# One-hot operands of a gate matrix made for eight tokens at a time, in slots shared with two tiles of the heads' stage

## Chip, cores and metric

The kernel runs on one core of one Trainium2 chip. The metric is the device time of one execution in microseconds (us). PE is TensorE, DVE is VectorE, ACT is ScalarE, POOL is GpSimd, and SP is the engine whose queue issues most of the DMAs.

## What is computed

One decoder block over 512 tokens of width 1024: a mixer (a depthwise convolution beside a sliding-window attention), and then a channel mixer that picks experts by product keys. The change lies in the second part, in float32 throughout:

```
def peer(h, w_pq, sub_keys, u_emb, v_emb):
    q = (h @ w_pq).reshape(B, S, PEER_HEADS, 2, PEER_DHALF)
    sc = jnp.einsum("bshcd,hcnd->bshcn", q, sub_keys)
    s_top, i_top = lax.top_k(sc, PEER_TOPK)                 # 16 of 128, twice per head
    cand = s_top[..., 0, :, None] + s_top[..., 1, None, :]
    cand_idx = i_top[..., 0, :, None] * N_KEYS + i_top[..., 1, None, :]
    best, pos = lax.top_k(cand, PEER_TOPK)                  # 16 of 256, per head
    expert_idx = jnp.take_along_axis(cand_idx, pos, axis=-1)
    gate = jax.nn.softmax(best, axis=-1)
    ...
    a = gelu(jnp.einsum("ced,cd->ce", u_emb[idx], hx))      # per token: 8 heads x 16 experts of 16384
    return jnp.einsum("ce,ced->cd", g * a, v_emb[idx])
```

## The kernel before

The 512 tokens are four blocks of 128. Block 0 takes its experts row by row: `gathered` (L634) fetches 128 rows of a table by an indirect DMA on POOL's queue, and DVE multiplies them (L651, L659). The other three blocks are dense: the product of all 16384 experts with all 384 tokens is formed on PE in 128 steps (`u_pieces`, L671, 24 matmuls of 384 columns each, with the weights split into a high and a low part by `load_w`, L128), multiplied by a gate matrix G, and multiplied with the second table (`v_products`, L698). G holds, for each token, the gate of each expert, and is nearly all zero.

The stages after the mixer, in order of time:

- **Heads** (`head`, L529, called eight times, 488 to 679 us). `scores` forms the queries (tile `pq`, L521, from PSUM by ACT) and multiplies them with the keys; DVE finds the top 16 (`top16`); `pick` (L548) looks the winners up through a one-hot tile `eq` (L569, one slot, twice per head) of 1024 elements per partition. Between the heads PE works on the first 25 `u_pieces`.
- **Gate stage** (`build_g`, L599, 684 to 847 us). Per block, `keys` (L584) transposes the indices, and `build_g` walks the 128 tokens. For each token G's 128 x 128 matrix is a product of two one-hot operands on PE (L628): `yt` marks the second key of each of the 128 chosen experts, `xt` the first key times the gate. DVE makes both: `yt` at L620 for `XT` = 4 tokens at once (512 elements per partition), `xt` at L623 likewise as a product of two narrow tiles `xa` and `xb`, which are made for 32 tokens at once (L612 twice, L614) in one slot each. `yt` and `xt` have two slots each (`XB` = 2). The four products of a group go to one PSUM tile of tag `sc` (two banks), ACT copies it into `gst` (L630), and after 16 tokens `gst` goes to DRAM (`gb`, L632, two slots). The choice between the tags `sc` and `ot` (L626) depends on the position within `XT` tokens in steps of four, so with four tokens it is always `sc`. After each group of four tokens 3.6 matmuls of the further `u_pieces` are threaded in (`U_PIECE`), so PE's queue alternates between a group of L628 and three or four matmuls of L146.
- **Loop over 128 steps** (from 847 us to the end). Per step: one `u_pieces`, a load of G's slice (`gl`, L685), its product with the experts' outputs (L690, L694, L695), `v_products` (L701 to L703), and about one gathered row of block 0 for DVE.

A scheduler orders the instructions of each engine at build time, and each engine runs its list in that order. Tiles are placed in pools; when the pools of the heads and the gate stage (`gp`, `rt`) are closed, the pools of the loop (`vp` with `gl`, `wh`, `wl`; `rows` with `hrow`, `acc` and the four slots of `row`) take the same memory, and a tile of theirs may be written once the tiles that lay there are released.

## Time and profile before

| | us |
|---|---|
| median of 3 runs | 1781.72 (1778.0 to 1785.92) |
| the profiled execution | 1780.86 |
| its span in the trace | 1779.1 |
| gate stage, first to last matmul of L628 | 684.1 to 845.9 |
| PE idle before matmuls of L628 | 12.2 |

The time of an execution holds its span and 1.8 us around it. A stage is read from the windows and the timeline: an engine's idle time there has a releaser in brackets, the instruction of another engine that ended it.

### The profile page before, as it was taken

To read this page: it belongs to the slowest core of one execution; us is meant where nothing else is said; L and a number is where in the kernel's file an instruction comes from. 1 tells how busy PE (TensorE), PEld (TensorE's weight loads), DVE (VectorE), ACT (ScalarE), POOL (GpSimd) and SP (SyncE) were. 2 spreads that over 40 slices of the span, in tenths; PEclk is the share of its full clock that TensorE was granted. 3 is DMA by queue.
4 is the path that set the end of the run, shared out by engine and by line. 5 is a ranking of instruction groups with operands and counts; after the bars stand their busy time and mean duration, and the time that the engine had idled before them with its cause. 6 is when DMAs were issued, how large, how long until landed. Compare 5 with 4: busy or idle time off the path is not lost. (4 is left out here: it accounts for less than half of the span.)

```text
span 1779.1 us, 25055 instructions
## 1 busy us (share of the span) xinstructions
PE 1708.0 (96%) x8892; PEld 1501.4 (84%) x8892; DVE 1366.0 (77%) x2755; ACT 905.6 (51%) x1287; POOL 458.6 (26%) x374
## 2 busy tenths in 40 slices
PE   7999999999999996999999999999999999989996
PEld 6887767788899996899999999999999999977775
DVE  6999994546689998888677777777768777768775
ACT  6449998644656656777333333333333333333332
POOL 1111010110111110001234434433535434434320
PEclk9999998999999998999999999999999999999998
DMA  8996553885999995878888889889979889878873
GB/s 243 229 220 152 131 129 74 188 225 177 259 217 218 212 210 153 257 240 263 300 318 316 318 282 325 316 287 321 322 275 326 309 295 337 302 267 302 299 259 127
DMA packets 165709, 444.86 MB, mean 250 GB/s; under 512 B 14544, under 2 KB 66256, under 8 KB 162512
## 3 DMA queue, kind: packets, MB, share of 16 engines
q0 software_dynamic: 53280, 194.01, 40.9%
q1 hardware_dynamic: 112304, 249.26, 39.2%
q8 instruction: 70, 1.15, 0.2%
q14 instruction: 55, 0.45, 0.1%
HBM read 410.44 MB, written 29.88 MB: 248 GB/s over the span
## 5 line engine op out<-in xcount | busy, mean ns | idle before, releaser
L131 ACT ACTIVATE whi<-wraw 128x1024 fp32r<-128x1024 f32 x346 | 365.3, 1057 | 358.1 <-PE mm L146 200.4
L146 PE MATMUL mm<-tTh,whi 128*128 128x384 f32 (+2 forms) x1168 | 398.5, 342 | 1.5 <-ACT wlo L134 1.4
L146 PE MATMUL mm<-tTl,whi 128*128 128x384 f32 (+2 forms) x1168 | 398.7, 342 | 0.2 <-DVE tTl L194 0.2
L137 DVE TENSOR_TENSOR wlo<-wraw,whi 128x1024 fp32r<-128x1024 f32 x232 | 282.5, 1221 | 63.1 <-ACT whi L131 55.9
L636 POOL DMA_INDIRECT row<-pv,eidx x128 | 181.2, 1416 | 275.9 <-DVE acc L659 259.9
L636 POOL DMA_INDIRECT row<-pu,eidx x128 | 178.2, 1392 | 265.4 <-DVE row L651 250.5
L694 ACT ACTIVATE wh<-gl 128x384 fp32r<-128x384 f32 x128 | 67.2, 526 | 345.8 <-PE ot L702 324.4
L146 PE MATMUL mm<-tTh,wlo 128*128 128x384 f32 (+2 forms) x1168 | 240.5, 341 | 0.0
L146 PEld LDWEIGHTS mm<-tTh,whi 128*128 128x128 f32 x1168 | 219.9, 188 | 9.9 <-ACT wlo L134 1.8
L146 PEld LDWEIGHTS mm<-tTl,whi 128*128 128x128 f32 x1168 | 219.8, 188 | 8.3 <-DVE tTl L194 0.4
L146 PEld LDWEIGHTS mm<-tTh,wlo 128*128 128x128 f32 x1168 | 202.9, 188 | 3.9
L659 DVE SCALAR_TENSOR_TENSOR acc<-row,gate,acc 128x1024 f32<-128x1024 f32 x128 | 163.9, 1280 | 12.9 <-DMA row<-pv,eidx 9.3
L296 DVE SCALAR_TENSOR_TENSOR yconv<-uc,pc,yconv 128x512 f32<-128x512 f32 x240 | 168.6, 741 | 0.4
L651 DVE SCALAR_TENSOR_TENSOR row<-row,hrow 128x1024 f32<-128x1024 f32 x128 | 154.2, 1219 | 7.7 <-DMA row<-pu,eidx 7.4
L146 PE MATMUL mm<-hTh,whi 128*128 128x512 f32 (+1 forms) x352 | 136.4, 390 | 1.1 <-ACT hTh L193 0.9
L146 PE MATMUL mm<-hTl,whi 128*128 128x512 f32 (+1 forms) x352 | 135.7, 388 | 1.4 <-DVE hTl L194 1.4
L695 DVE TENSOR_TENSOR wl<-gl,wh 128x384 fp32r<-128x384 f32 x128 | 70.9, 554 | 76.6 <-ACT wh L694 76.6
L134 ACT ACTIVATE wlo<-whi 128x1024 fp32r<-128x1024 f32 x114 | 120.1, 1054 | 9.7 <-PE mm L146 9.0
L690 DVE TENSOR_TENSOR gl<-gl,ga 128x384 f32<-128x384 f32 x128 | 61.9, 552 | 80.5 <-DMA gl<-gb 80.5
L630 ACT ACTIVATE gst<-sc 128x512 f32<-128x512 f32 x96 | 100.9, 1075 | 33.8 <-PE sc L628 27.7
L628 PE MATMUL sc<-xt,yt 128*128 128x128 f32 x768 | 103.2, 278 | 12.2 <-DVE xt L623 9.3
L628 PEld LDWEIGHTS sc<-xt,yt 128*128 128x128 f32 x768 | 99.1, 193 | 16.3 <-ACT gst L630 10.2
(252 smaller groups left out, 3107.9 us busy)
## 6 DMA issues: line engine op xcount, KB each, us to landing
wraw<-put SPq DMA_DIRECT2D x128, 512.0 KB, 5.5
wraw<-pv SPq DMA_DIRECT2D x128, 512.0 KB, 5.8
gb<-gst SPq DMA_DIRECT2D x24, 1024.0 KB, 5.5
gl<-gb SPq DMA_DIRECT2D x48, 512.0 KB, 7.1
wraw<-w_in SPq DMA_DIRECT2D x42, 512.0 KB, 4.8
wlo<-put POOLq DMA_DIRECT2D x42, 512.0 KB, 7.2
wlo<-w_in POOLq DMA_DIRECT2D x40, 512.0 KB, 6.0
wraw<-w_out SPq DMA_DIRECT2D x16, 512.0 KB, 3.4
```

Of the source, the lines that this page charges most:

```text
L131: nc.scalar.activation(hi, raw, AF.Copy)
L134: nc.scalar.activation(lo, hi.bitcast(F32), AF.Copy, scale=-1.0)
L137: nc.vector.tensor_tensor(lo, raw, hi.bitcast(F32), op=OP.subtract)
L146: pace[0] = nc.tensor.matmul(p, v[:, k * P:(k + 1) * P], t, start=(n == 0), stop=(n == len(terms) - 1))
L296: nc.vector.scalar_tensor_tensor(y[:, j], uc[:, t:t + S], w, y[:, j], op0=OP.mult, op1=OP.add)
L628: nc.tensor.matmul(p[:, t], yt[:, t1 + t], xt[:, t1 + t].rearrange("p a b -> p (a b)"), start=True, stop=True)
L630: nc.scalar.activation(st[:, :, t0 + t1:t0 + t1 + 4].rearrange("p i t -> p t i"), p, AF.Copy)
L636: ins = nc.gpsimd.indirect_dma_start(out=r, out_offset=None, in_=table, in_offset=bass.IndirectOffsetOnAxis(ap=eidx[:, ROW_CHUNKS.index(b) ...
L651: nc.vector.scalar_tensor_tensor(r, r, 1.0, h, op0=OP.mult, op1=OP.mult, accum_out=dots[:, s:s + 1])
L659: nc.vector.scalar_tensor_tensor(acc, r, gate[:, b, s:s + 1], acc, op0=OP.mult, op1=OP.add)
L694: nc.scalar.activation(wh3, w, AF.Copy)
L695: nc.vector.tensor_tensor(wl3, w, wh3.bitcast(F32), op=OP.subtract)
```

## The change

`XT` becomes 8: one instruction of DVE makes `yt` for eight tokens, one makes `xt`, of 1024 elements per partition each. The inner loop over steps of four tokens then runs twice per group, so the PSUM tiles alternate between `sc` and `ot`, two banks each. `yt` and `xt` keep two slots, of 4 KB per partition each instead of 2 KB. To make room, the heads' `pq` takes the slots of `xt`, and `eq` the slots of `yt` (two, where it had one); the memory of both pools together stays the same, but the tiles' places in it move.

```
-XT = 4
+XT = 8
...
-        q = rt.tile([P, S], F32, name="pq", bufs=2)
+        q = gp.tile([P, S], F32, name="pq", tag="xt", bufs=XB)
...
-            eq = rt.tile(wide, F32, name="eq")
+            eq = gp.tile(wide, F32, name="eq", tag="yt", bufs=XB)
...
-                yt = gp.tile([P, XT, P], F32, name="yt", bufs=XB)
+                yt = gp.tile([P, XT, P], F32, name="yt", tag="yt", bufs=XB)
...
-                xt = gp.tile([P, XT, high, LOW], F32, name="xt", bufs=XB)
+                xt = gp.tile([P, XT, high, LOW], F32, name="xt", tag="xt", bufs=XB)
```

The places move as follows, in bytes of a partition: `xt` and `yt` now lie at 176896 to 193280, in front of `xa`, `xb` and `gst` (`gst` at 196352 to 212736, before at 179968 to 196352). The first slot of `gl` (176896 to 189184) lay over `xa`, `xb` and both slots of `gst`, and lies now over `xt` and the first slot of `yt`. `hrow` and `acc` (207616 to 211712) and the first slot of `row` (211712 to 215808) lay over tiles of the heads, and lie now over the second slot of `gst` (and `sel`).

DVE's list at the third border between two blocks of 32 tokens (`xa` and `xb` belong to the new block). Before:

```order
L620 TENSOR_TENSOR yt<-keyT,iota 128x512
L623 TENSOR_TENSOR xt<-xa,xb 128x512
L612 TENSOR_TENSOR xa<-keyT,iota 128x256
L612 TENSOR_TENSOR xb<-keyT,iota 128x512
L620 TENSOR_TENSOR yt<-keyT,iota 128x512
L614 TENSOR_TENSOR xa<-xa,gT 128x256
L620 TENSOR_TENSOR yt<-keyT,iota 128x512
L623 TENSOR_TENSOR xt<-xa,xb 128x512 x2
```

The same place in the changed kernel:

```order
L620 TENSOR_TENSOR yt<-keyT,iota 128x1024
L623 TENSOR_TENSOR xt<-xa,xb 128x1024
L612 TENSOR_TENSOR xa<-keyT,iota 128x256
L612 TENSOR_TENSOR xb<-keyT,iota 128x512
L620 TENSOR_TENSOR yt<-keyT,iota 128x1024
L614 TENSOR_TENSOR xa<-xa,gT 128x256
L623 TENSOR_TENSOR xt<-xa,xb 128x1024
L620 TENSOR_TENSOR yt<-keyT,iota 128x1024
```

Before, two `yt` stand ahead of the block's first `xt` at each of the eleven borders of the stage (at five of them one stands ahead of `xa` already); now one does. PE's list keeps its order; only the PSUM tags alternate.

DVE's list at the start of the gate stage, before:

```order
L612 TENSOR_TENSOR xa<-keyT,iota 128x256
L612 TENSOR_TENSOR xb<-keyT,iota 128x512
L620 TENSOR_TENSOR yt<-keyT,iota 128x512 x2
L592 CAST k_p<-k_u 128x128
L614 TENSOR_TENSOR xa<-xa,gT 128x256
L593 SCALAR_TENSOR_TENSOR k_q<-k_p,sel 128x128
L623 TENSOR_TENSOR xt<-xa,xb 128x512 x2
```

In the changed kernel:

```order
L612 TENSOR_TENSOR xa<-keyT,iota 128x256
L612 TENSOR_TENSOR xb<-keyT,iota 128x512
L620 TENSOR_TENSOR yt<-keyT,iota 128x1024 x2
L592 CAST k_p<-k_u 128x128
L614 TENSOR_TENSOR xa<-xa,gT 128x256
L593 SCALAR_TENSOR_TENSOR k_q<-k_p,sel 128x128
L623 TENSOR_TENSOR xt<-xa,xb 128x1024 x2
```

The order is the same, each `yt` and `xt` being twice as long; PE's first L628 waits for the first `xt` of this list.

SP's queue at the end of the gate stage, before:

```order
L632 DMA gb_82<-gst 128x2048 x2
L125 DMA wraw<-put 128x1024
L647 DMA hrow<-h2d_79 128x1024
L632 DMA gb_82<-gst 128x2048 x2
L125 DMA wraw<-pv 128x1024
L632 DMA gb_82<-gst 128x2048
L125 DMA wraw<-put 128x1024
L685 DMA gl<-gb_80 128x8x128
L685 DMA gl<-gb_81 128x8x128
L685 DMA gl<-gb_82 128x8x128
```

In the changed kernel (`gb_80`, `gb_81` and `gb_82` are the gate matrices of the three blocks in DRAM, `h2d_79` block 0's input):

```order
L632 DMA gb_82<-gst 128x2048 x2
L125 DMA wraw<-put 128x1024
L632 DMA gb_82<-gst 128x2048 x2
L125 DMA wraw<-pv 128x1024
L632 DMA gb_82<-gst 128x2048
L125 DMA wraw<-put 128x1024
L685 DMA gl<-gb_80 128x8x128
L685 DMA gl<-gb_81 128x8x128
L685 DMA gl<-gb_82 128x8x128
L647 DMA hrow<-h2d_79 128x1024
```

The load of `hrow` moves from before the last three stores of the gate matrix to behind its first three loads.

## Rows read from the trace of the kernel before

**Rows 1.** The page's part 1, busy time of each engine over the whole span, its share of the span, and its instructions.

```profile
PE 1708.0 (96%) x8892; PEld 1501.4 (84%) x8892; DVE 1366.0 (77%) x2755; ACT 905.6 (51%) x1287; POOL 458.6 (26%) x374
```

**Rows 2.** Busy time of each engine by stretch: from and to, length, then PE, PEld, DVE, ACT and POOL with their instructions, the granted TensorE clock, the DMA engines' share and GB/s. The first two are the end of the last head and the start of the gate matrix, the third is the gate stage, the last two are the loop behind it.

```profile
670.00:680.00 10.00, 1.18 (x5) 0.78 (x5) 9.73 (x27) 1.98 (x5) 0.87 (x1) 0.66 0.61 140
680.00:690.00 10.00, 8.14 (x44) 7.12 (x44) 7.58 (x17) 4.17 (x7) 0.00 (x0) 0.66 0.00 0
684.00:847.00 163.00, 150.80 (x1117) 147.00 (x1117) 136.38 (x223) 128.99 (x140) 15.78 (x17) 0.99 0.77 241
1000.00:1300.00 300.00, 300.00 (x1519) 273.21 (x1518) 224.78 (x321) 109.43 (x147) 128.19 (x92) 1.00 0.88 310
1300.00:1600.00 300.00, 295.19 (x1468) 266.36 (x1468) 227.04 (x237) 104.42 (x142) 124.49 (x89) 0.99 0.85 304
```

**Rows 3.** Who waited for whom from 684 to 850 us: total us, times, longest us.

```profile
DVE yt L620 <- PE sc L628: 21.4, 51, 1.6
...
PE sc L628 <- DVE xt L623: 9.3, 9, 1.2
...
PE sc L628 <- ACT gst L630: 2.9, 3, 1.2
```

**Rows 4.** The timeline of PE in the gate stage, those matmuls of L628 before which PE stood idle (start us, us, instruction, count, and in brackets the idle time with what ended it): the first two of the twelve, and the last.

```profile
698.88 1.13 PE L628 MATMUL sc<-xt,yt 128*128 128x128 f32 x8 [1.24 <-DVE xt L623]
...
708.68 1.16 PE L628 MATMUL sc<-xt,yt 128*128 128x128 f32 x8 [0.37 <-ACT gst L630]
...
834.27 0.91 PE L628 MATMUL sc<-xt,yt 128*128 128x128 f32 x6 [1.25 <-ACT gst L630]
```

**Rows 5.** The timeline of PE and DVE from 720 to 730 us, over the border between two blocks of 32 tokens (same columns; rows of PE's loads, of ACT and most of L146 are left out).

```profile
720.60 1.05 PE L628 MATMUL sc<-xt,yt 128*128 128x128 f32 x8
...
722.18 1.05 PE L628 MATMUL sc<-xt,yt 128*128 128x128 f32 x8
...
723.01 0.42 DVE L612 TENSOR_TENSOR xa<-keyT,iota 128x256 f32<-128x256 f32 x1
...
723.36 0.68 DVE L612 TENSOR_TENSOR xb<-keyT,iota 128x512 f32<-128x512 f32 x1
...
723.60 1.05 PE L628 MATMUL sc<-xt,yt 128*128 128x128 f32 x8
723.96 0.68 DVE L620 TENSOR_TENSOR yt<-keyT,iota 128x512 f32<-128x512 f32 x1
...
724.56 0.42 DVE L614 TENSOR_TENSOR xa<-xa,gT 128x256 f32<-128x256 f32 x1
...
724.90 0.68 DVE L620 TENSOR_TENSOR yt<-keyT,iota 128x512 f32<-128x512 f32 x1
725.02 0.34 PE L146 MATMUL mm<-tTl,whi 128*128 128x384 f32 x1
725.50 1.28 DVE L623 TENSOR_TENSOR xt<-xa,xb 128x512 f32<-128x512 f32 x2
...
726.33 1.13 PE L628 MATMUL sc<-xt,yt 128*128 128x128 f32 x8 [0.97 <-DVE xt L623]
...
728.01 1.05 PE L628 MATMUL sc<-xt,yt 128*128 128x128 f32 x8
...
729.10 0.69 DVE L620 TENSOR_TENSOR yt<-keyT,iota 128x512 f32<-128x512 f32 x1 [0.31 <-PE sc L628]
...
729.71 0.68 DVE L623 TENSOR_TENSOR xt<-xa,xb 128x512 f32<-128x512 f32 x1
```

**Rows 6.** The timeline at the start of the gate stage.

```profile
678.79 0.48 PE L596 MATMUL tr<-ident,k_p 128*128 128x128 f32 x1 [10.15 <-DVE k_p L592]
...
681.44 1.28 DVE L620 TENSOR_TENSOR yt<-keyT,iota 128x512 f32<-128x512 f32 x2
682.64 0.22 DVE L592 CAST k_p<-k_u 128x128 f32<-128x128 uint32 x1
...
683.32 1.28 DVE L623 TENSOR_TENSOR xt<-xa,xb 128x512 f32<-128x512 f32 x2
...
684.05 2.07 PE L628 MATMUL sc<-xt,yt 128*128 128x128 f32 x8
...
686.88 1.05 PE L628 MATMUL sc<-xt,yt 128*128 128x128 f32 x8
```

**Rows 7.** The timeline of DVE in the last head: a tensor_tensor of 1024 elements, and what DVE starts next.

```profile
674.85 1.22 DVE L570 TENSOR_TENSOR eq<-c_j,iota 128x1024 f32<-128x1024 f32 x1
675.99 0.22 DVE L590 CAST k_u<-sel 128x128 uint32<-128x128 f32 x1
```

**Rows 8.** The timeline of POOL, SP's queue, PE and DVE where the gate stage hands over to the loop behind it: the first gather, the last store of the gate matrix, its first loads, the first product with them, and the first use of a gathered row.

```profile
836.71 1.05 POOL L636 DMA_INDIRECT row<-pu,eidx  x1 [0.30 <-issue]
...
847.30 0.32 SPq L632 DMA_DIRECT2D gb<-gst  x1
...
855.70 7.42 SPq L685 DMA_DIRECT2D gl<-gb  x6
...
864.67 0.50 PE L701 MATMUL tr<-whi,wh 128*128 128x512 f32 x1 [1.16 <-ACT wh L694]
...
874.69 1.21 DVE L651 SCALAR_TENSOR_TENSOR row<-row,hrow 128x1024 f32<-128x1024 f32 x1
```

**Rows 9.** The gathers of L636: us from the end of an issue to the landing of its rows.

```profile
DMA to landing us min/median/max: 4.1/6.9/10.5
```
## The prediction

> **What bounds the kernel now.** First the busy line of the page: PE works 96% of the span, DVE 77% [rows 1]. Then the same by stretch [rows 2]: in the loop PE is busy 300.00 of 300 us, at the higher of its two clock levels (granted clock 1.00, 2.4 GHz), so what an earlier stage saves there moves everything behind it forward. PE is not full in the gate stage, the only one whose instructions the change lengthens or shortens: 150.80 us busy of 163. So the reader's next view is who waits there [rows 3]: PE's L628 waited for DVE's `xt` 9 times, 9.3 us in all, and 3 times for ACT, 2.9 us, together 12.2 us. But DVE waited for PE as well, 51 times, 21.4 us: each waits for the other, so DVE has the time but not at the right moment. The timeline says which moment [rows 4, 5]: the waits stand some 13.5 us apart, one at each of the eleven borders between blocks of 32 tokens, and one more of 0.37 us at 708.68. Two of the three that are put down to ACT (the last is at 834.27) are such borders too, of the same size.
>
> At a border [rows 5] DVE makes `xa` (723.01), `xb` (723.36), `yt` (723.96), `xa` times the gate (724.56), another `yt` (724.90) and then the two `xt` (725.50), while PE has run out of finished groups. PE's groups start 1.58 us apart with four matmuls of L146 between (720.60, 722.18) and 1.42 with three (722.18, 723.60). The last L146 starts at 725.02, so the next group was due at 723.60 + 1.58 = 725.18. It starts at 726.33, 1.15 us late; the trace counts 0.97 of that as idle and the other 0.18 as the modelled end of the last matmul.
>
> **A border, worked out before and after.** DVE's pitches, from start to start [rows 5]: `xa` 0.35, `xb` 0.60, `xa` times the gate 0.34, `yt` 0.60 to 0.61, and `xt` 0.68 to its end. A group's slots come free 1.09 us after PE starts it (728.01 to 729.10). With PE's mean pitch of 1.5 us a slot freed by one group is needed again two groups later: 2 x 1.5 - 1.09 = 1.91 us. DVE needs 0.61 + 0.68 + 0.05 = 1.34, a margin of 0.57, and idles about 0.2 per group (1.5 - 0.61 - 0.68). The border adds 0.35 + 0.60 + 0.34 = 1.29 and the second `yt` 0.61, 1.90 in all; less the idle 0.2 and the margin 0.57 that is 1.13 us late, and 1.15 was measured. So the sum describes the stage.
>
> With eight tokens a `yt` or `xt` has 1024 elements. Such an operation of the same kind took 1.22 us, and DVE's next started after 1.14 [rows 7]. A pair then costs 1.14 + 1.22 + 0.05 = 2.41 us instead of two of 1.34. PE's period per group is 3.00 to 3.16. The slot of a group comes free 1.09 us into its second half; from that half's start to the start of the group after next are 1.42 to 1.58 and a whole period, so 4.42 at least, which leaves DVE 3.33 and a margin of 0.92. Its idle time per group is 3.0 - 2 x 1.14, about 0.7, and `xa` and `xb` need no slot of PE's, so they run in it. The border adds 1.29, with no second `yt`; 1.29 - 0.7 = 0.6 late against a margin of 0.92, and PE waits for nothing, with 0.3 to spare. **Gain: 11.8 us idle at the eleven borders (12.2 less 0.37) and 0.17 each behind the modelled ends, 13.7 us.**
>
> If DVE could not run `xa` and `xb` ahead, each border would keep 1.29 - 0.92 = 0.37 us, 4.1 in all. That is the lower bound of this gain, 9.6.
>
> **The start of the stage.** PE is idle here for 10.15 us before its first transposes, and the granted clock is 0.66 on average [rows 2, 6], so part of it at the lower level of 1.2 GHz. The first L628 waits for the first `xt`, which stands behind two `yt`. These took 1.20 (681.44 to 682.64) and will take 2 x 1.14 = 2.28, 1.08 more; the first `xt` takes 1.22 instead of 0.68, 0.54 more. PE starts 1.6 us later, and nothing wins that back, since PE is the bound from there on. Group and first three L146 take 2.83 us at the low clock (684.05 to 686.88) against 1.42 later on; that stays, unless the longer pause adds a second such group, 1.4 us. **Cost 1.6, between 1.1 (the `yt` alone) and 3.0.**
>
> Here a rule speaks against the change. The rows show PE waiting for DVE while DVE idles 21.4 us of the stage [rows 3]. The Trainium skill, page Perfetto Trace Analysis, section Optimizing Scalar/DVE Operations, has it that where such an engine is not saturated but makes bubbles on others, breaking up its instructions may let work finish sooner. By that rule the doubled `xt` would make each border later, where the rows give 13.7 us of gain; the start, as worked out, is a case of it. It is the third rival below.
>
> **Edits with one answer.** PSUM has four banks for the products instead of two, so ACT may fall three groups behind before PE waits; that can take the 0.37 at 708.68 and is set to nothing. ACT works 128.99 of 163 us [rows 2]; in 151 that is 85%, so it doesn't become the bound. `pq` keeps two slots, which the first `xt` finds read long before; `eq` gets a second one, which only lets DVE put one lookup ahead of a reduction. Both are free.
>
> **The hand-over to the loop.** The new places of the tiles change two waits [rows 8]. The first load of G's slice went out at 855.70, after the last store (847.30) had landed, because its slot lay over both of `gst`. It now lies over `xt` and `yt`, so two of its three loads may go before; the third still waits. PE idled 1.16 us there (864.67), which may go. Against it, the first gather (836.71) now waits for the last store too, about 19.0 us (to the moment of 855.70), and `hrow` behind it: four gathers of 0.5 MB then share the DMA engines with the loads, which at 310 GB/s [rows 2] is up to 6.8 us. The first gathered row was used at 874.69, 38 us after the first gather. 12 us earlier and with the gather 19 later some 19 us are left (874.69 - 855.70), against 6.9 from issue to landing, 10.5 at most [rows 9]. I take nothing for both, with -1.2 and +6.8 as ends.
>
> **Sum**, against the profiled execution of 1780.86 us: 1780.86 - 13.7 + 1.6 = **1768.8, said as 1769**, 0.7% less. The median of three runs is 0.9 above that execution, within its spread.
>
> **Rivals.**
>
> *Double operations, half the gain.* DVE doesn't get ahead at a border, because a group of 1024 is begun only when its whole slot is free. Then 4.1 us of waits stay, and the start costs its 3.0: 1780.9 - 9.6 + 3.0 = 1774.3. For it: the start shows exactly that, and the spare of 0.3 us rests on pitches of other instructions. Against it: `xa` and `xb` wait for no slot, and DVE idles 0.7 per group.
>
> *Given back in the loop.* The loop is held by something that doesn't move with PE, the DMA engines at 0.85 to 0.88 busy; then the time stays near 1779. Against it: PE's 300.00 of 300 [rows 2].
>
> *Slower, at the borders.* PE starts a group only when its whole `xt` is there, and the first `xt` of a block is 0.54 longer (1.22 against 0.68). If the borders stay as late as now and this comes on top, they cost 11 x 0.54 = 5.9 more: 1780.9 + 5.9 + 1.6 = 1788.4. It decides from 1.0 us late per border on (now 1.15, less the 1.6 of the start spread over eleven). This is what the rule on breaking up instructions would make of it. Against it: the second `yt` is gone from the way, and the margin grows from 0.57 to 0.92; for it, that the same did happen at the start.
>
> *Slower, in the loop.* The gathers lose their head start. If the first row lands more than 19 us after its issue, DVE stands at its L651 in a fixed list, behind which the low parts of the weights and of G (L137, L695) wait, and PE for these. If the whole 19.0 us are lost and never regained, 1768.8 + 19.0 = 1787.8; from 12.1 lost on the kernel is slower than before. Against it: landings of 10.5 us at most.
>
> **How the numbers follow.** 0.5% of this kernel, 8.9 us, is about what a measurement can tell from no change, so faster means below 1772.8. The forecast gets 0.68, with 0.93 of it below that line; half the gain 0.18, of which a third falls below; given back 0.07; the two slower ones 0.03 and 0.04. Faster: 0.63 + 0.06 = 0.69. The slower ones lie 0.4% above, so half of them, 0.04, counts as slower by over 0.5% (above 1790.6); the rest, 0.27, is within 0.5%. The range: downward 13.7 - 1.1 + 1.2 = 13.8 gives 1767.1, and the runs before reach 3.7 below their median, 1763; upward the half gain, 1774.3, and the same 3.7, 1778. It leaves out the last three rivals, 0.14, and little of the others.
>
> **What would show it.** In the profile after: 48 `yt` and 48 `xt` of 1.22 us; PE idle before L628 below 2 us in the stage; the stage's first L628 1.6 us later against the last transposes, and the stage shorter by 12; PE's first idle in the loop still near 1 us, the first L651 without a wait for its row. It is wrong if PE still waits at the borders for `xt` (the first rival, or with over 1.0 us each the third), if the stage is 12 shorter and the end isn't (the second), or if DVE waits for rows at its first L651 (the fourth).

## The result, and the profile after

| | before | after |
|---|---|---|
| median, us | 1781.8 (1778.0 to 1785.92, 4 runs) | 1771.46 (1768.11 to 1772.01, 4 runs) |
| ratio of the times, 95% interval | | 0.9935 (0.9919 to 0.9951) |
| profiled execution, span | 1780.86, 1779.1 | 1772.01, 1770.2 |

The changed kernel is 0.65% faster, 10.3 us by the medians and 8.9 between the two profiled executions. 1769 was forecast, 1763 to 1778 as the range. The gain came out 2.5 us smaller than forecast by the medians, 3.2 between the profiled executions, but terms inside the sum did not come out as they were priced, and they partly cancel.

The page's part 1 of the kernel after, which answers [rows 1]:

```profile
PE 1707.9 (96%) x8892; PEld 1504.4 (85%) x8892; DVE 1355.1 (77%) x2659; ACT 898.5 (51%) x1287; POOL 461.3 (26%) x374
```

PE does the same work in a span 8.9 us shorter; DVE's instructions fell by 96, which are the 48 `yt` and 48 `xt` that were merged away. Busy time by stretch, in the columns of [rows 2]: the gate stage, three pieces of the hand-over, and the loop.

```profile
684.00:835.00 151.00, 149.22 (x1119) 148.67 (x1120) 128.02 (x132) 122.60 (x140) 11.26 (x13) 0.98 0.80 253
850.00:855.00 5.00, 1.68 (x10) 1.35 (x8) 0.00 (x0) 0.00 (x0) 0.00 (x0) 1.00 0.99 343
855.00:862.00 7.00, 5.07 (x12) 4.05 (x13) 6.29 (x12) 2.27 (x4) 0.00 (x0) 0.51 0.91 287
1000.00:1300.00 300.00, 300.00 (x1518) 273.05 (x1517) 224.55 (x319) 108.87 (x146) 125.17 (x91) 1.00 0.88 310
```

The gate stage is full now (149.22 of 151 us; before, 150.80 of 163). The second and third rows are the surprise: from 850 to 855 PE stands idle for 3.3 of 5 us while the DMA engines are 0.99 busy, and from 855 to 862 it works at a granted clock of 0.51, about the lower level of 1.2 GHz.

Who waited for whom, in the columns of [rows 3], from 684 us to the end of the hand-over:

```profile
DVE yt L620 <- PE ot L628: 18.5, 24, 3.6
ACT gst L630 <- DMA gb<-gst: 18.0, 14, 2.5
...
PE tr L701 <- ACT wh L694: 5.3, 1, 5.3
...
PE sc L628 <- DVE xt L623: 0.4, 1, 0.4
```

Of PE's 12.2 us before L628, 0.4 are left, at the start. The eleven border waits are gone and so are the waits for ACT. ACT now waits 18.0 us for stores of `gst`, and nobody waits for that. In their place stands one wait of 5.3 us before the loop's first L701, where [rows 8] had 1.16.

A border, from the timelines of PE and DVE (the place that answers [rows 5]; rows of L146 are left out):

```profile
720.12 1.22 DVE L623 TENSOR_TENSOR xt<-xa,xb 128x1024 f32<-128x1024 f32 x1
720.88 1.05 PE L628 MATMUL ot<-xt,yt 128*128 128x128 f32 x8
721.37 0.42 DVE L612 TENSOR_TENSOR xa<-keyT,iota 128x256 f32<-128x256 f32 x1
721.71 0.68 DVE L612 TENSOR_TENSOR xb<-keyT,iota 128x512 f32<-128x512 f32 x1
722.31 1.22 DVE L620 TENSOR_TENSOR yt<-keyT,iota 128x1024 f32<-128x1024 f32 x1
722.47 1.05 PE L628 MATMUL sc<-xt,yt 128*128 128x128 f32 x8
723.45 0.42 DVE L614 TENSOR_TENSOR xa<-xa,gT 128x256 f32<-128x256 f32 x1
723.88 1.05 PE L628 MATMUL ot<-xt,yt 128*128 128x128 f32 x8
723.90 1.23 DVE L623 TENSOR_TENSOR xt<-xa,xb 128x1024 f32<-128x1024 f32 x1
...
725.47 1.05 PE L628 MATMUL sc<-xt,yt 128*128 128x128 f32 x8
```

While PE works on the pair at 722.47 and 723.88, DVE finishes the next block's narrow tiles and makes its first `yt` and its first `xt`, which ends at 725.13, 0.34 us before PE takes it at 725.47 without a wait. The prediction had 0.3 to spare. At the eleven borders the first `xt` is ready 0.27 to 0.47 us ahead; where PE did wait for one before the change, it started 0.14 to 0.15 us behind its end, so what is left to spare is 0.1 to 0.3.

The start of the stage, which answers [rows 6]:

```profile
680.05 0.47 PE L596 MATMUL tr<-ident,k_p 128*128 128x128 f32 x1 [10.23 <-DVE k_p L592]
...
682.70 2.35 DVE L620 TENSOR_TENSOR yt<-keyT,iota 128x1024 f32<-128x1024 f32 x2
...
685.64 2.35 DVE L623 TENSOR_TENSOR xt<-xa,xb 128x1024 f32<-128x1024 f32 x2
...
686.92 2.08 PE L628 MATMUL sc<-xt,yt 128*128 128x128 f32 x8 [0.44 <-DVE xt L623]
```

From the first transposes to the first L628 it takes 6.87 us instead of 5.26: 1.61 more, for 1.6 predicted.

The hand-over, from the timelines of SP's queue, POOL, DVE and PE, which answers [rows 8]: the last store of the gate matrix, the loads of G's slice in two threes with `hrow` between, the first gather, the first work of DVE and of PE with the slice, and the first use of a row.

```profile
835.46 0.32 SPq L632 DMA_DIRECT2D gb<-gst  x1
...
839.23 4.07 SPq L685 DMA_DIRECT2D gl<-gb  x3
840.53 1.05 POOL L636 DMA_INDIRECT row<-pu,eidx  x1 [13.73 <-DMA gb<-gst]
843.35 7.64 SPq L647 DMA_DIRECT2D hrow<-h2d  x1
...
851.04 5.81 SPq L685 DMA_DIRECT2D gl<-gb  x3
...
855.72 3.84 DVE L690 TENSOR_TENSOR gl<-gl,ga 128x384 f32<-128x384 f32 x8 [8.62 <-DMA gl<-gb]
856.93 0.80 PE L701 MATMUL tr<-whi,wh 128*128 128x512 f32 x1 [5.26 <-ACT wh L694]
...
868.03 1.23 DVE L651 SCALAR_TENSOR_TENSOR row<-row,hrow 128x1024 f32<-128x1024 f32 x1
```

The loads go out 3.8 us after the last store instead of 8.4, and yet from that store to DVE's first L690 it takes 20.26 us, where before it took 16.21 (847.30 in [rows 8], to this row):

```profile
863.51 3.84 DVE L690 TENSOR_TENSOR gl<-gl,ga 128x384 f32<-128x384 f32 x8 [4.57 <-DMA gl<-gb]
```

The four gathers now stand right beside the loads. The first row is there without a wait (868.03).

**Where the time went, by marks on PE's timeline.** The marks are the first transposes of the stage, the third group of L628 (by then two groups have run at the low clock), the last group, the first L701, and the first L701 of the loop's second step. Differences between the two profiled executions, us:

| stretch | before | after | difference |
|---|---|---|---|
| to the first transposes | 678.79 | 680.05 | +1.26 |
| to the third group | 9.69 | 12.07 | +2.38 |
| to the last group | 156.64 | 141.16 | -15.48 |
| to the first L701 | 19.55 | 23.65 | +4.10 |
| first step of the loop | 6.69 | 9.03 | +2.34 |
| rest of the loop | 907.74 | 904.24 | -3.50 |
| sum | 1779.1 | 1770.2 | -8.9 |

So the stage gave 15.5 us, and the hand-over took back 6.4: 4.1 more idle, and 2.3 because PE came out of a 5.26 us pause at the lower clock.

### The profile page after: what moved, and what is told of

Read it like the earlier page. It is cut to its first block, busy times and chain, and to the rows that moved or that the text cites. A ratio compares the mean times of both kernels' runs of the same rounds, so it can differ in the third digit from the quotient of the medians.

```text
span 1770.2 us, 24879 instructions
## 1 busy us (share of the span) xinstructions
PE 1707.9 (96%) x8892; PEld 1504.4 (85%) x8892; DVE 1355.1 (77%) x2659; ACT 898.5 (51%) x1287; POOL 461.3 (26%) x374
## 5 line engine op out<-in xcount | busy, mean ns | idle before, releaser
L146 PE MATMUL mm<-tTh,whi 128*128 128x384 f32 (+2 forms) x1168 | 398.4, 342 | 1.5 <-ACT wlo L134 1.4
L146 PE MATMUL mm<-tTl,whi 128*128 128x384 f32 (+2 forms) x1168 | 398.6, 342 | 0.2 <-DVE tTl L194 0.2
L636 POOL DMA_INDIRECT row<-pv,eidx x128 | 185.6, 1450 | 268.4 <-DVE acc L659 257.7
L636 POOL DMA_INDIRECT row<-pu,eidx x128 | 176.5, 1379 | 271.3 <-DVE row L651 243.3
L146 PE MATMUL mm<-tTh,wlo 128*128 128x384 f32 (+2 forms) x1168 | 240.5, 341 | 0.1
L146 PEld LDWEIGHTS mm<-tTh,whi 128*128 128x128 f32 x1168 | 220.0, 188 | 10.0 <-ACT wlo L134 1.8
L146 PEld LDWEIGHTS mm<-tTl,whi 128*128 128x128 f32 x1168 | 219.8, 188 | 8.3 <-DVE tTl L194 0.4
L146 PEld LDWEIGHTS mm<-tTh,wlo 128*128 128x128 f32 x1168 | 202.9, 188 | 4.2 <-DMA wlo<-w_pq 0.3
L659 DVE SCALAR_TENSOR_TENSOR acc<-row,gate,acc 128x1024 f32<-128x1024 f32 x128 | 164.0, 1282 | 12.3 <-DMA row<-pv,eidx 7.7
L651 DVE SCALAR_TENSOR_TENSOR row<-row,hrow 128x1024 f32<-128x1024 f32 x128 | 154.4, 1220 | 8.6 <-DMA row<-pu,eidx 8.0
L146 PE MATMUL mm<-hTh,whi 128*128 128x512 f32 (+1 forms) x352 | 136.7, 391 | 1.1 <-ACT hTh L193 0.8
L146 PE MATMUL mm<-hTl,whi 128*128 128x512 f32 (+1 forms) x352 | 136.1, 389 | 1.4 <-DVE hTl L194 1.4
L690 DVE TENSOR_TENSOR gl<-gl,ga 128x384 f32<-128x384 f32 x128 | 62.0, 553 | 88.6 <-DMA gl<-gb 88.6
L695 DVE TENSOR_TENSOR wl<-gl,wh 128x384 fp32r<-128x384 f32 x128 | 71.0, 555 | 67.9 <-ACT wh L694 63.2
L701 PE MATMUL tr<-whi,wh 128*128 128x512 f32 x256 | 101.2, 397 | 9.1 <-ACT wh L694 5.3
L135 POOL DMA_DIRECT2D wlo<-w_in x40 | 34.9, 872 | 268.6 <-ACT wlo L134 212.3
L703 PE MATMUL tr<-whi,wl 128*128 128x512 f32 x256 | 96.4, 402 | 8.3 <-DVE wl L695 8.3
```

What stands on the lines that cost most here:

```text
L146: pace[0] = nc.tensor.matmul(p, v[:, k * P:(k + 1) * P], t, start=(n == 0), stop=(n == len(terms) - 1))
L636: ins = nc.gpsimd.indirect_dma_start(out=r, out_offset=None, in_=table, in_offset=bass.IndirectOffsetOnAxis(ap=eidx[:, ROW_CHUNKS.index(b) ...
L651: nc.vector.scalar_tensor_tensor(r, r, 1.0, h, op0=OP.mult, op1=OP.mult, accum_out=dots[:, s:s + 1])
L659: nc.vector.scalar_tensor_tensor(acc, r, gate[:, b, s:s + 1], acc, op0=OP.mult, op1=OP.add)
L695: nc.vector.tensor_tensor(wl3, w, wh3.bitcast(F32), op=OP.subtract)
L701: nc.tensor.matmul(p, w[0][:, chunk(n)], v[0][:, ns], start=(i == 0), stop=False)
```

## The experiments

All ratios are to the kernel before, measured beside each run. The same stretches for every run, from its profiled execution. That is one execution of several: in run 1 it lies 4.6 us below the run's median, in runs 8, 9 and 11 2.8, 5.4 and 4.0 above it.

| kernel | median us | ratio (95%) | transposes to third group | third to last group | last group to L701 (idle) | first step | rest |
|---|---|---|---|---|---|---|---|
| before | 1781.8 | | 9.69 | 156.64 | 19.55 (1.16) | 6.69 | 907.74 |
| after | 1771.46 | 0.9935 (0.9919-0.9951) | 12.07 | 141.16 | 23.65 (5.26) | 9.03 | 904.24 |
| 1 four banks alone | 1782.13 | 1.0000 (0.9990-1.0010) | 9.61 | 155.81 | 19.19 (0.80) | 6.74 | 905.59 |
| 2 eight tokens, two banks | 1778.11 | 0.9979 (0.9968-0.9990) | 11.22 | 146.07 | 23.16 (4.77) | 8.15 | 906.62 |
| 3 four tokens, four slots | 1773.62 | 0.9951 (0.9939-0.9963) | 11.04 | 146.27 | 20.26 (1.87) | 6.71 | 904.93 |
| 4 `gst` in front | 1774.89 | 0.9951 (0.9938-0.9964) | 12.19 | 141.16 | 22.58 (4.18) | 8.02 | 909.55 |
| 5 `hrow` early | 1771.6 | 0.9949 (0.9935-0.9962) | 11.33 | 141.16 | 22.01 (3.62) | 9.42 | 904.54 |
| 6 start in fours | 1770.97 | 0.9932 (0.9919-0.9946) | 10.31 | 141.16 | 22.25 (3.85) | 8.03 | 906.13 |
| 7 = 6 and 4 | 1767.94 | 0.9933 (0.9918-0.9948) | 9.87 | 141.24 | 22.61 (4.21) | 9.06 | 904.02 |
| 8 gathers held back | 1774.12 | 0.9952 (0.9940-0.9964) | 11.84 | 141.96 | 18.25 (0) | 6.61 | 915.23 |
| 9 = 8 and 6 | 1770.47 | 0.9931 (0.9920-0.9943) | 10.87 | 141.16 | 18.22 (0) | 6.61 | 915.83 |
| 10 before, gathers late | 1787.24 | 1.0026 (1.0017-1.0036) | 9.80 | 156.48 | 22.35 (3.95) | 8.28 | 908.37 |
| 11 two gathers held | 1776.4 | 0.9973 (0.9964-0.9983) | 11.71 | 141.17 | 20.60 (2.21) | 8.27 | 915.49 |
| 12 = 11 and 6 | 1773.87 | 0.9953 (0.9940-0.9966) | 10.44 | 141.16 | 19.63 (1.24) | 6.69 | 911.55 |

### The stage: depth, size or banks

**1. The kernel before with four PSUM banks.** Groups of four tokens and all places as before, only the tags alternate.

```
-                    p = psum(("sc", "ot")[t1 // 4 % 2])...
+                    p = psum(("sc", "ot")[(t0 + t1) // 4 % 2])...
```

> The kernel before with one part of the change alone: groups of four tokens, but their PSUM tiles alternate between sc and ot, four banks instead of two. Theory 'ahead' (the waits at the eleven borders went because DVE works two groups of eight tokens ahead): the border waits on xt stay, about 11.8 us idle before L628, and only the 0.37 us wait for ACT at 708.68 goes; time 1781 (1779 to 1784). Rival 'banks' (ACT's evictions held PE at the borders and the four banks let it run): idle before L628 under 2 us, time 1766 to 1768.

The waits of PE from 684 to 850 us:

```profile
PE sc L628 <- DVE xt L623: 9.4, 9, 1.2
PE sc L628 <- ACT gst L630: 2.5, 2, 1.2
```

The small wait of [rows 4] at 708.68 is gone, the eleven borders stand, and the time is that of before (ratio 1.000). Banks alone are worth 0.8 us of the stretch. The two waits put down to ACT are borders, as the prediction read them: two more banks don't move them.

**2. The changed kernel with two banks.**

```
-                    p = psum(("sc", "ot")[t1 // 4 % 2])...
+                    p = psum("sc")...
```

> The changed kernel with the PSUM tiles of all groups on sc alone, two banks. 'Ahead': no wait at the borders, some waits of under 0.5 us for ACT where two of its other operations fall between two evictions, 2 us in all at most; time 1771 to 1774. 'Banks': the waits come back, over 10 us idle before L628, time over 1781.

The waits of PE in the same stretch:

```profile
PE sc L628 <- ACT gst L630: 2.8, 6, 1.1
PE sc L628 <- DVE xt L623: 0.4, 1, 0.4
```

No border wait is left, but six waits for ACT have come (2.8 us; with what each costs behind the modelled ends, the stretch is 4.9 longer than in the changed kernel). 2 us at most and 1771 to 1774 were expected; the time is 1778.11. With two banks ACT must have copied a group before PE may start the next but one, and ACT is held up now and then. Four of the six end behind such a row of ACT's timeline (the others of these rows start at 742.35, 773.45 and 786.20):

```profile
711.31 1.96 ACT L630 ACTIVATE gst<-sc 128x512 f32<-128x512 f32 x2 [0.98 <-DMA gb<-gst]
```

`gst` has two slots, and ACT may not write into one until its store has landed; the groups that PE finishes meanwhile pile up in PSUM. With four banks ACT waits 18.0 us for these stores and PE never notices. The kernel before had the small wait at 708.68 only. I read it so that PE, standing still at each border, rarely got far enough ahead to run into ACT; it fits with run 1, which gained nothing.

**3. Four tokens as before, but four slots each of `yt` and `xt`, on two banks.** The lead is 16 tokens as in the changed kernel; the instructions are small.

```
-XT = 8
-XB = 2
+XT = 4
+XB = 4
...
-            eq = gp.tile(wide, F32, name="eq", tag="yt", bufs=XB)
+            eq = gp.tile(wide, F32, name="eq", tag="gst", bufs=2)
...
-            st = gp.tile([P, P, GT], F32, name="gst", bufs=2)
+            st = gp.tile([P, P, GT], F32, name="gst", tag="gst", bufs=2)
...
-                    p = psum(("sc", "ot")[t1 // 4 % 2])...
+                    p = psum("sc")...
```

> Groups of four tokens as in the kernel before (XT 4, 512 elements, PSUM on sc alone), but four slots each for yt and xt (XB 4), so DVE may again be sixteen tokens ahead with twice as many instructions; pq in the slots of xt, eq in those of gst. 'Ahead': no waits for xt at the borders, idle before L628 under 2 us; the first L628 waits behind four yt of 512, 4 x 0.61 = 2.4 us instead of 1.2, so the start costs 1.2 us or, with the low clock held longer, 2; time 1767 to 1772. Rival 'fewer instructions' (the gain is DVE's saved fixed cost, 130.8 us of yt and xt before against 117.3 after): DVE's busy time is as before and so are the borders, 10 us idle or more, time 1780 to 1783.

```profile
PE sc L628 <- ACT gst L630: 3.0, 6, 1.1
```

This is all that PE waits for in L628, and third to last group take 146.27 us against 146.07 in run 2. So the border waits are removed by the lead of DVE, not by larger or fewer instructions. On two banks the lead gives 10.4 of the 15.5 us (156.64 to 146.27) and the banks then 5; the other way round the banks give 0.8 (run 1) and the lead then 14.65 (155.81 to 141.16). The two parts need each other. With the same lead the small instructions leave more to spare: the first `xt` of a block is ready 1.9 to 2.8 us ahead here. The time, 1773.62, lies 1.6 above the 1772 that was expected at most, since these waits for ACT had not been counted.

### The start

**6. The first eight tokens as two groups of four, the rest as changed.**

```
-            for t0 in range(0, GT, XT):
+            t0 = 0
+            while t0 < GT:
+                XT = 4 if n == 0 and g == 0 and t0 < 8 else 8
...
+                t0 += XT
```

> The changed kernel, but the first eight tokens of the stage are made as two groups of four; all others by eight. Theory 'start' (the doubled operations delay the first L628 by 1.6 us, and the longer pause leaves PE at its lower clock for more work, 0.8 us): the first L628 comes 5.3 us behind the first transposes instead of 6.9, the third group 9.7 us behind them instead of 12.1, time 1769 (1767.5 to 1771). Rival: the time won at the start is lost again at the first border or the hand-over, time 1771 to 1772.

The first group on PE's timeline:

```profile
681.32 0.47 PE L596 MATMUL tr<-ident,k_p 128*128 128x128 f32 x1 [10.22 <-DVE k_p L592]
...
686.58 2.08 PE L630 MATMUL sc<-xt,yt 128*128 128x128 f32 x8
```

From the transposes to the first L628 it takes 5.26 us, exactly as before the change, so the 1.61 are the two long `yt` and the long `xt`. The third group comes 10.31 us behind the transposes instead of the 9.7 that was expected. The median fell by 0.5 only; a difference of 1.6 us is at the edge of what these runs resolve, and the timeline decides it.

### The hand-over

**4. `gst` in a pool in front, so that the slots of `row` and `hrow` lie elsewhere and the first gathers need not wait for the last store.** (`gl` then lies over `gst` again, as before the change.)

```
+    gs = gctx.enter_context(tc.tile_pool(name="gs", bufs=1, reuse_waits="tile"))
...
-            st = gp.tile([P, P, GT], F32, name="gst", bufs=2)
+            st = gs.tile([P, P, GT], F32, name="gst", bufs=2)
```

> The changed kernel with gst in a pool of its own in front of the others, so that gl lies over gst again and hrow and the first slot of row over yt, xa, xb and sel instead of gst. Theory 'gathers' (the 5.26 us that PE idles before the first L701, against 1.16 before, come from the first gathers, which now start with the landing of the last store and share the DMA engines with the first loads of G): the first gather goes out some 6 us earlier than now against the last L628, PE's idle before the first L701 falls to 1 to 3 us, time 1767 to 1770. Rival 'shorter stage' (the stage now ends sooner, so less of PE's other work is left to cover the way through DRAM, wherever the tiles lie): idle stays at 4 to 6 us, time 1770 to 1773.

```profile
831.41 1.04 POOL L637 DMA_INDIRECT row<-pu,eidx  x1 [2.92 <-DMA gb<-gst]
...
836.02 0.32 SPq L633 DMA_DIRECT2D gb<-gst  x1
...
847.54 7.32 SPq L686 DMA_DIRECT2D gl<-gb  x6
```

The gathers start 9 us earlier, and the idle time before L701 stays (4.18). The rows show why: the last store now takes 11.5 us until the loads behind it start (836.02 to 847.54), against 8.4 in [rows 8]. The gathers' bytes fell on the store instead of on the loads. Its time, 1774.89, lies above what either theory gave.

**5. `hrow` in the slot of a tile that is free early, so that it leaves the place between the loads.**

```
-            h = rows.tile([P, D], F32, name="hrow", tag="acc")
+            h = keep.tile([P, D], F32, name="hrow", tag="g")
...
```

> The changed kernel with hrow in the slot of g (free since the second norm; the last norm's g is loaded behind the last dot product instead), so its load leaves the place in SP's queue between the first three loads of G and the next. The gathers still wait for the last store. Theory 'gathers': PE's idle before the first L701 stays at 4 to 6 us, time 1770 to 1773. Rival 'queue' (the load of hrow in SP's queue is what holds the loads of G): idle falls to 1 to 2 us, time 1767 to 1769.

PE's idle time before L701 is 3.62, just below the 4 to 6 of the theory 'gathers': `hrow`'s place is at most 1.6 of the 5.26, and run 6, which keeps it, has 3.85. So the place in SP's queue isn't what it hangs on; the first step of the loop, 9.42, is the longest of all.

**7. Runs 4 and 6 together.**

> The edits of the start in fours and of gst in front together. If both terms are what I hold them for, 2.4 us at the start and 2 to 4 at the hand-over: time 1765 to 1767, 15 us under the kernel before. If the hand-over doesn't depend on the places: 1769.

Its median, 1767.94, is the lowest of all and lies between the two forecasts, but the interval of its ratio (0.9918 to 0.9948) holds the changed kernel's; idle before L701 is 4.21, so the hand-over did not gain.

What was open after these: are the gathers the cause, or is a stage that ends 15 us sooner simply followed by a longer stretch of transfers? Run 4 alone seemed to speak for the second. Three runs decide it.

**8. The changed kernel with the four gathers held back behind the first loads of G's slice**, by one small copy on POOL's queue that reads them.

```
+    held = small.tile([P, 1], F32, name="held", bufs=1)
...
+        if i == 0:
+            nc.gpsimd.tensor_copy(held, gl[0][:, ND * NG - 1, GI - 1, 0:1])
```

> The changed kernel, but GpSimd's queue gets one tiny copy that reads the first slot of gl, in front of the first four gathers, so these go out only when the first loads of G's slice have landed. 'Contention': in the changed kernel the four gathers (2.1 MB, 840.5 us on) share the DMA engines with the loads of G's slice, and that, not the loads' start, makes the idle time before the first L701; without them the loads land about 8 us after the last store, idle falls from 5.26 to 1-1.7 us, the first step of the loop (first L701 to the next step's) takes 6.7 us again instead of 9.0, and the time is about 1765.5 (1764-1767.5). 'Shorter stage': the stores and loads are as slow by themselves since the stage hands them over faster; idle stays at 3.6-5.3 us and the time at 1770-1772.

The copy, the first L701 and the first row, then two of PE's waits from 850 us to the end and one of DVE's from 854 us:

```profile
851.12 0.18 POOL L768 COPY held<-gl 128x1 f32<-128x1 f32 x1 [23.39 <-DMA gl<-gb]
...
853.26 0.39 PE L701 MATMUL tr<-whi,wh 128*128 128x512 f32 x1
...
865.91 1.22 DVE L651 SCALAR_TENSOR_TENSOR row<-row,hrow 128x1024 f32<-128x1024 f32 x1
```

```profile
PE tr L703 <- DVE wl L695: 13.7, 4, 4.1
...
PE tr L702 <- DVE wlo L137: 1.9, 2, 1.6
```

```profile
DVE gl L690 <- DMA gl<-gb: 102.8, 15, 10.3
```

Without the gathers the loads land in time: PE doesn't wait at all before L701, and the first step is 6.61 us. Up to there "contention" is right, and by more than I expected. But the time is 1774.12, not 1765.5, because the rest of the loop is 11.0 us longer than in the changed kernel (915.23 against 904.24). The first row is used 6.0 us after the second step's first L701 (859.87 to 865.91), against 2.1 in the changed kernel. PE, which waited for nothing from the second step to the 89th in any of the ten kernels whose gathers aren't held behind these loads, now waits for DVE twice there, and more in the last steps. What was gained at the hand-over is given back.

How much is given back is less sure than 11.0: this execution is 2.8 us above the run's median, and the changed kernel's is among the shorter of those ten (904.0 to 909.6). By the medians, runs 8, 9, 11 and 12 lose some 5 to 10 us behind the hand-over against the kernels that they were made from. It isn't the clock: the records of this execution give 0.95, neither of the two levels, also where the others give 1.00, and yet from the second step to the 57th it took the same 448.56 us as the ten. Nor is it a wait for the rows themselves. Of DVE's waits it is L690's for the loads of G's slice that set the held kernels apart, 102.8 us here and 96.8 to 102.8 in the four, against 76.0 to 87.2 in the ten; L651's waits for rows are 11.1 to 14.2 against 3.5 to 12.3. That a DVE which is later in its fixed list (some two rows per step, 256 over 128 steps) lets the slots of `gl` come free later, and so their loads, is how I read it; no run shows it.

**9. The same with the first eight tokens in fours.**

> The gathers held back as in the run beside it, and the first eight tokens as two groups of four. If the two gains add ('contention'), 1.6 us less than with the gathers held alone, about 1764 (1762-1766). By 'shorter stage' 1768-1771.

PE's idle time before L701 is 0, the first step 6.61 and the rest 915.83, in an execution that is 5.4 us above the run's median. The median, 1770.47, is no better than that of run 6 without the hold (ratios 0.9931 and 0.9932), though the hand-over and the first step are 5.4 us shorter: the same bill.

**10. The kernel before, with its gathers held until the last store has landed.** Its stage is as long as ever (156.48).

```
+            if b == BUILT[-1] and g == NG - 1:
+                nc.gpsimd.memset(st[:, 0, 0:1], 0.0)
```

> The kernel before, with one tiny memset on GpSimd's queue in front of the first four gathers that waits for the last store of gst, so the gathers go out together with the loads of G's slice, 19 us later than before. 'Contention': idle before the first L701 rises from 1.16 to 4-6 us, the first step of the loop takes 8-9.4 us instead of 6.7, and the time rises by 4-7 us, to about 1787 (1785.5-1789). 'Shorter stage': the stage is as long as before, so idle stays at 0.8-1.5 us and the time within 1 us of before.

```profile
848.48 0.32 SPq L632 DMA_DIRECT2D gb<-gst  x1
...
853.59 13.51 SPq L687 DMA_DIRECT2D gl<-gb  x6
854.27 1.04 POOL L638 DMA_INDIRECT row<-pu,eidx  x1 [0.70 <-issue]
...
867.48 3.84 DVE L692 TENSOR_TENSOR gl<-gl,ga 128x384 f32<-128x384 f32 x8 [7.36 <-DMA gl<-gb]
868.65 0.50 PE L703 MATMUL tr<-whi,wh 128*128 128x512 f32 x1 [3.95 <-ACT wh L696]
```

This settles it. Six loads that took SP 7.42 us to issue in [rows 8] take 13.51 with the gathers beside them; idle rises from 1.16 to 3.95 and the first step from 6.69 to 8.28, in a stage that is not shorter, and the kernel is 4 to 5 us slower (ratio 1.0026, 1.0017 to 1.0036). "Shorter stage" falls. The store shows the other side: from it to the first load are 5.1 us here (848.48 to 853.59) and 8.4 in [rows 8], where the gathers went out beside the last stores.

Runs 2 and 3 say the same with stages of equal length (146.07 and 146.27). In run 2 the gathers wait for the last store as in the changed kernel. In run 3 the tiles' places differ again, and the first gather waits only for a matmul of the stage; two rows of run 3:

```profile
836.76 1.04 POOL L636 DMA_INDIRECT row<-pu,eidx  x1 [5.38 <-PE sc L628]
...
840.77 0.32 SPq L632 DMA_DIRECT2D gb<-gst  x1
```

It goes out 4.0 us ahead of the last store, the first load of G's slice 3.9 behind it (844.63), so the loads are not held up as in run 4. Idle is 1.87 instead of 4.77, the first step 6.71 instead of 8.15, and the rest of the loop is not longer (904.93): 4.3 us of the hand-over are saved. These places with four banks were not tried.

**11 and 12. Only the third and fourth gather held back; 12 with the start in fours.**

```
...
+                if s == 2:
+                    c = nc.gpsimd.tensor_copy(held, gl[0][:, ND * NG - 1, GI - 1, 0:1])
+                    tc.add_manual_dep(c.ins, rowins[1].ins.name, ...)
...
```

> The changed kernel, with the copy that waits for the first loads of G's slice between the second and the third gather, so two gathers (1 MB) share the DMA engines with these loads instead of four, and the other two follow. 'Contention' in proportion: idle before the first L701 1-3 us instead of 5.26, the first step of the loop 6.7-8 us instead of 9.0, so 3-6 us less up to there; and since the first two rows are there in time, DVE doesn't fall behind and the rest of the loop costs what it costs in the changed kernel: about 1767 (1765-1769.5). If the rest of the loop is lost by any gather that comes later ('late rows'), it is 4-11 us longer, as with all four held, and the time 1771-1774.

> The same with the first eight tokens as two groups of four: 1.6 us less than the run beside it, 1765.5 (1763.5-1768) by 'contention', 1769-1772 by 'late rows'.

Two waits of PE in run 11, at the hand-over and in the middle of the loop:

```profile
854.84 0.50 PE L709 MATMUL tr<-whi,wh 128*128 128x512 f32 x1 [2.21 <-ACT wh L702]
...
1391.21 0.50 PE L710 MATMUL tr<-wlo,wh 128*128 128x512 f32 x1 [3.23 <-DVE wlo L137]
```

Idle falls in proportion (2.21 and 1.24), as contention has it, but the rest of the loop stays long (915.49 and 911.55), which is what "late rows" forecast; both times lie above the ranges of either theory. Run 11 is slower than the changed kernel, from which it was made; run 12 is 2.9 us above run 6 by the medians, with intervals that overlap. In these two the last L690 of the first eight also moved behind others in DVE's list, so their rest of the loop isn't the hold alone.

No version of these is shown to beat the changed kernel: after, 6, 7 and 9 lie at 0.9931 to 0.9935, within each other's intervals.

## Why the prediction was right, and where it was not

**Borders: right, and the sum undersized by 1.8.** -13.7 was forecast; third to last group measured -15.48. The mechanism is as worked out: eight tokens per slot let DVE run `xa`, `xb` and a whole `yt` ahead, with 0.34 us to spare at the border shown. Start to start, over PE's usual pitch, the eleven borders had cost 13.6 us (1.1 to 1.4 each), as the sum has it; of the other 1.8, 0.8 are what the banks give alone (run 1). The rival that DVE would not get ahead falls, and with it the one that would be slower at the borders. The Trainium skill (page Perfetto Trace Analysis, section Optimizing Scalar/DVE Operations) has it that where an unsaturated engine makes bubbles on others, breaking up its instructions may let work finish sooner. That was set beside the rival that is slower at the borders; there the trace shows the opposite of what it would give: instructions twice as long, 12.2 us of waits gone. Run 3 shows that the size isn't what makes PE wait there, but how far the engine can run ahead. At the start the rule holds, and splitting the first group took the 1.61 back.

**"PSUM has four banks ... is set to nothing": the step that failed inside this sum.** It was priced by the one wait of 0.37 us that the trace of before showed. Alone the banks are indeed worth next to nothing (0.8 in run 1), but without the border waits they are worth 5 us (146.07 and 146.27 with two banks, 141.16 with four). A wait that is absent from a trace can be absent because another wait stands in front of it. The total is near all the same, because the lead alone gave only 10.4 of the 13.7: the sum took it that nothing else would hold PE up, and the banks, which it counted for nothing, made that so. That much is luck.

**Start: right, 1.61 for 1.6.** From the first to the third group it took 5.20 us instead of 4.43, within the low-clock stretch. Run 2, which makes the same two groups, took 4.36 there, and over all runs it is 4.4 to 5.6, so those 0.8 us aren't tied to the change.

**"The hand-over ... I take nothing for both": mis-sized by 6.4.** The mechanism stands in the prediction, with its upper end of +6.8: the gathers lose their head start and share the DMA engines with the loads. I set it against the loads' earlier start and called it even. What I missed: the first product needs all three loads and the third waits for the last store anyway, so the earlier start gains nothing (20.26 us from the last store to the first L690, against 19.00 in run 10, whose loads all wait for that store), and the stall also costs clock. A check on the size: four gathers of 0.5 MB are 2.1 MB. From 846 to 850 us before the change, with the last stores and the gathers both under way, the DMA engines moved 422 GB/s:

```profile
846.00:850.00 4.00, 4.00 (x25) 4.00 (x24) 0.61 (x1) 2.61 (x3) 0.00 (x0) 1.00 1.01 422
```

At that rate the gathers occupy 5.0 us, at the 343 GB/s of 850 to 855 us after the change 6.1; 5.26 is what holding them back took away. The Trainium skill, page HBM Reference, section Specifications (TRN2), has a core streaming alone at about 425 GB/s. The 422 agree.

**Rest of the loop: -3.50, not shown to be the change's.** The kernels before and after take the same 710.04 us from the second step to the 89th, so the rival that the loop would give the gain back falls. All of the 3.5 is in the last 39, where PE waits for L695 and L695 behind loads of G's slice: 10.9 us in four waits before, 8.3 after. In the ten kernels whose gathers aren't held behind the loads of G's slice the rest of the loop scatters from 904.0 to 909.6, with a mean of 907.2 for before, 1 and 10, which have the old places, and 905.7 for the other seven. I take it for scatter. Why the last steps scatter was not tried.

**Before the stage: +1.26.** 0.81 of it is there at 458 us already (the first matmul of the heads' weights starts at 457.92 before, 458.73 after), where the lists are the same. The traces settle what the moved `pq` and `eq` cost: from the first product of the queries with the keys, the first reader of `pq`, to the first transposes it takes 205.34 or 205.35 us in before and runs 1 and 10, and 205.40 or 205.41 in the kernels with the moved tiles (205.51 and 205.61 in runs 9 and 8), so some 0.07 us. "Both are free" was right. All the rest lies ahead of that product, which comes at 473.46 before, 474.65 after, and 473.4 to 477.2 in all; why it scatters was not tried.

**The fourth rival** (slower in the loop through late rows) didn't happen, since PE stood still at the hand-over and the first row met DVE without a wait. Runs 8, 9, 11 and 12 show that it was a near thing: there the first row was used 6.0 to 7.5 us after the second step's first L701, and the rest of the loop was longer. In the ten others it was 1.0 to 5.3 us (5.3 in run 3), and PE waited for nothing before the 89th step.

**The sum, term by term.** Between the profiled executions -8.9 came for -12.1. The stage gave 1.8 more than forecast at the borders and 0.8 less up to the third group, the hand-over took 6.4, the stretch ahead of the stage 1.3, and the rest of the loop gave 3.5. Without the last, which is taken for scatter, the gain would be 5.4: that the time lies near the forecast is in part luck.

## What to carry to other kernels

When two engines take turns waiting for each other at regular places, count how far the producer can run ahead at such a place, in items that the consumer needs, and not the length of its instructions; and price the next wait in line (here ACT, behind its stores, on two banks) as if the first were gone. A change of a tile's place in memory is a change of transfers: list which DMAs it lets go earlier or later, add up their bytes against what the DMA engines moved in the same stretch, and put that on the path when PE has work for less time than they take. Moving such bytes about gains little when every neighbour is on somebody's path: right ahead of a store that all loads wait for they hit the store (run 4), beside the loads they hit these, and behind them they hit the loop. The place that cost least was in run 3, ahead of the last store with only the loads' own data waiting for it.

## What was not expected of the hardware

In eight executions PE paused 2.21 to 5.26 us before the loop (after, runs 2, 4, 5, 6, 7, 10, 11). Behind the pause the granted clock fell to about its lower level, 1.2 GHz (0.51 in the changed kernel from 855 to 862 us, 0.50 in run 7 from 852 to 856, 0.60 on average in run 11 from 856 to 860), and the first step took 8.0 to 9.4 us. In the six with pauses of 0 to 1.87 us (before, runs 1, 3, 8, 9, 12) the step took 6.6 to 6.7 us, and the granted clock of runs 3 and 12 stayed at 1.00. So the 5.26 us pause cost 2.3 us beyond itself. The extra time doesn't grow evenly with the pause: it is the largest, 2.7 us, after the 3.62 of run 5. From the second step to the 89th none of the ten kernels without a hold behind the loads differs from another by over 0.01 us: a loop that PE fills takes the same time in every execution, and all scatter of this kernel lies around it.
